# A transformer block and an RWKV/convolution block on one core: feed-forward activation sums behind the next products, GpSimd's 1024-column operations in two halves, the convolution norm's sums at a later place on TensorE

## The chip, the core and the metric

The kernel runs on 1 core of one Trainium2 chip. Its time is the device time of one execution in microseconds (us); lower is better. The engines are TensorE (PE, with its weight loads as PEld), VectorE (DVE), ScalarE (ACT), GpSimd (POOL) and SyncE (SP, which here only issues DMAs). Each has a queue of instructions that it works off in order; they meet through semaphores.

## What is computed

Two blocks stand one behind the other on 512 tokens of 1024 channels, all in f32. The first has two layers, each an attention mixer, a layer norm, a feed-forward with a squared ReLU, another layer norm and a gated embedding. The second is an RWKV-7 mixer beside a convolution branch, then a feed-forward of the same form. What the change touches is this:

```python
def _sq_relu_mlp(x, w_up, w_down):                 # layers 0 and 1: 1024 -> 4096 -> 1024
    return jnp.square(jax.nn.relu(x @ w_up)) @ w_down
...
    x = x + jnp.square(jax.nn.relu(h2 @ w_ff1[l])) @ w_ff2[l]      # second block
...
def _layernorm(x, g, b):                           # in the convolution branch
    mu = jnp.mean(xf, axis=-1, keepdims=True)
    var = jnp.mean(jnp.square(xf - mu), axis=-1, keepdims=True)
    y = (xf - mu) * lax.rsqrt(var + LN_EPS)
```

## The kernel before, in words

**Splits.** Each f32 operand is split into a rounded part `hi` and a rest `lo`, and a product is three matmuls, hi·hi, hi·lo and lo·hi (`mm3`, L290 to L292). A weight arrives by DMA in a tile `wraw` of 128x1024 (`load_part`, L261), ScalarE copies it to `whi`, and the rest `wlo` is made in one of three ways: VectorE or GpSimd subtracts (L273 in `load_part`, L389 in `split_sb`), or ScalarE negates and a DMA adds (L270, L271).

**Feed-forward** (`ffn`, three times: from about 225, 930 and 2115 us on). The 4096 hidden columns are worked off in 16 pieces of 256. `up(i)` makes one piece: two products of 24 matmuls each into PSUM (`psm`, two banks), and for each ScalarE applies ReLU (L440) and square (L441) into the tile `F` (`hf`, 128 x 8 x 256). From `F` VectorE makes four sums of blocks (L448 to L451; L451 needs L449's result), ScalarE rounds blocks 0 to 2 and blocks 3 to 6 into `hh` (L388, 128x768 and 128x1024), and VectorE makes the rests `hl` (L389). `F` has one buffer: the next piece's ReLU waits until the last rest of the piece before has been read.

`down(u)` multiplies two pieces with 512 rows of the second weight by a scheme of seven block products, for which GpSimd makes four sums of weight quarters (L488, L489, L490, L493, each 128x1024) and some of the rests. The products go through four PSUM banks `psa`; VectorE adds each result to `x` (L458, L460) or to a partial sum `q` (L505) and so frees its bank. The last 512 rows are done plainly (`down_last`).

**Order of the work.** The source is not the order of execution: the framework's scheduler places the instructions on each engine by its own estimate of their times, and the queues then run in that order. The order listings below show it.

**Convolution norm.** The convolution branch's layer norm (`ConvNorm`) sums eight tiles over the channels on GpSimd while they are made (L1345); `mean` is one matmul with ones (L1350) into the single PSUM bank `psd`. `center` then takes the eight tiles in turn: load from DRAM, subtract on GpSimd (L1357), store, square on ScalarE (L1359), add on GpSimd (L1363). `var` is a second matmul with ones into `psd` (L1368), a root on ScalarE and a reciprocal on VectorE. `sums()` (L1179) steps through these in stage 7 of `second_mixer`, woven by `interleave` with the other streams of that stage; a `yield` gives the weight of a step, and the number in `work += [(12.7, sums())]` sets the pace. `norm` then overwrites the shared activations `H` with the result, which is possible once the last of stage 8's gate products (`branch_gate`, also in `psd`) has read them. Beside all this runs `wkv_chunks`, a recurrence of eight steps for each of eight column groups; one step goes from TensorE (`psq`, L1416) to VectorE (L1655) to TensorE (L1661) to VectorE (L1663) to TensorE and to VectorE (L1675).

Of the kernel before, what the change touches and what calls it, by code (L numbers as in the profile page):

```python
# [11 lines left out]
F32 = mybir.dt.float32  # L12
F32R = mybir.dt.float32r
AF = mybir.ActivationFunctionType
ALU = mybir.AluOpType
# [185 lines left out]
class Ctx:  # L201
# [59 lines left out]
    def load_part(self, ap, raw, hi, lo, eng):  # L261

        nc = self.nc
        m = ap.shape[0] // 128 * ap.shape[1]
        nc.sync.dma_start(raw[:, :m].rearrange("p (k n) -> p k n", n=ap.shape[1]),
                          ap.rearrange("(k p) n -> p k n", p=128))
        nc.scalar.activation(hi[:, :m], raw[:, :m], AF.Copy)  # L267
        if eng is None:

            nc.scalar.activation(lo[:, :m], hi[:, :m].bitcast(F32), AF.Copy, scale=-1.0)  # L270
            nc.gpsimd.dma_start(lo[:, :m].bitcast(F32), raw[:, :m], accum_op=ALU.add)  # L271
        else:
            eng.tensor_tensor(lo[:, :m], raw[:, :m], hi[:, :m].bitcast(F32), op=ALU.subtract)  # L273

    def psum(self, st, **tags):

# [109 lines left out]

def split_sb(g, src, hi, lo, eng=None):
    g.nc.scalar.activation(hi, src, AF.Copy)  # L388
    (eng or g.nc.gpsimd).tensor_tensor(lo, src, hi.bitcast(F32), op=ALU.subtract)  # L389


def split_ps(g, ps, hi, lo):
# [10 lines left out]
def ffn(g, w_up, w_down, X, alpha, hp, tmp, late, norm, fm=None, fill=None):  # L403

    nc = g.nc
    V = nc.vector
    units = w_up.shape[1] // 512
    h = []
    seen = set()
    Q1 = [g.ps("psu") for _ in range(2)]
    QS = {k: hp.tile([128, 2, 512], F32, name=f"q{k}", tag=f"q{k}", bufs=1) for k in (5, 6, 7)}

    def first_two(W):

        pss = [g.ps("psa") for _ in range(2)]
        for half, t in enumerate(HALF_TOKENS):
            for e, ps in enumerate(pss):
                for kc in range(8):
                    w = tuple(a[:, e * 128:e * 128 + 128] for a in W[kc])
                    mm3(nc, ps[:, t], w, (X[0][:, kc, t], X[1][:, kc, t]), kc == 0, kc == 7)
                if half == 0:
                    late[e]()
        return pss

    def up(i):

        plain = i // 2 == units - 1
        W = g.load_w(w_up[:, i * 256:i * 256 + 256], eng=nc.gpsimd if i > 1 else None)
        F = tmp.tile([128, 8, 256], F32, name="hf", tag="hf")
        pss = first_two(W) if i == 0 else None
        for e in range(2):
            p3 = (pss[e] if pss else proj_fm(g, W, X, e * 128)).rearrange("p (a t) -> p a t", a=2)
            o = F[:, 1:3, :] if e else F[:, 0:8:7, :]
            nc.scalar.activation(o, p3, AF.Relu)  # L440
            nc.scalar.activation(o, o, AF.Square)  # L441
        hh = hp.tile([128, 7, 256], F32R, name="hh", tag="hh")
        hl = hp.tile([128, 7, 256], F32R, name="hl", tag="hl")
        split_sb(g, F[:, 0:3, :], hh[:, 0:3, :], hl[:, 0:3, :], V)
        if plain:
            split_sb(g, F[:, 7, :], hh[:, 3, :], hl[:, 3, :], V)
        else:
            V.tensor_tensor(F[:, 3, :], F[:, 7, :], F[:, 2, :], op=ALU.add)  # L448
            V.tensor_tensor(F[:, 4, :], F[:, 3, :], F[:, 0, :], op=ALU.subtract)  # L449
            V.tensor_tensor(F[:, 5, :], F[:, 0, :], F[:, 7, :], op=ALU.subtract)  # L450
            V.tensor_tensor(F[:, 6, :], F[:, 1, :], F[:, 4, :], op=ALU.subtract)  # L451
            split_sb(g, F[:, 3:7, :], hh[:, 3:7, :], hl[:, 3:7, :], V)
        h.append((hh, hl))

    def add(tb, c, ps):
        xs = g.x[tb][:, c * 512:c * 512 + 512]
        if (tb, c) not in seen and alpha != 1.0:
            V.scalar_tensor_tensor(xs, xs, alpha, ps, op0=ALU.mult, op1=ALU.add)  # L458
        else:
            V.tensor_tensor(xs, ps, xs, op=ALU.add)  # L460
        seen.add((tb, c))

    def down(u):
        q = w_down[u * 512:u * 512 + 512, :].rearrange("(j e p) n -> e p j n", e=2, p=128)
        new = lambda: g.wraw.tile([128, 1024], F32, name="wraw", tag="wraw")

        def quarter(e, c):
            t = new()
            nc.sync.dma_start(t.rearrange("p (j n) -> p j n", j=2), q[e][:, :, c * 512:c * 512 + 512])
            return t  # L470

        def parts(t, eng=None):
            hi = g.whi.tile([128, 1024], F32R, name="whi", tag="whi")
            lo = g.wlo.tile([128, 1024], F32R, name="wlo", tag="wlo")
            split_sb(g, t, hi, lo, eng)
            return hi, lo

        def product(W, k, ps, first=True, last=True):
            for t in range(2):
                for j in range(2):  # L480
                    x = tuple(a[:, k, t * 128:t * 128 + 128] for a in h[2 * u + j])
                    w = tuple(a[:, j * 512:j * 512 + 512] for a in W)
                    mm3(nc, ps[t], x, w, first and j == 0, last and j == 1)

        b11, b21, b12, b22 = quarter(0, 0), quarter(1, 0), quarter(0, 1), quarter(1, 1)
        B11, B21 = parts(b11), parts(b21)
        t3 = new()
        nc.gpsimd.tensor_tensor(t3, b22, b12, op=ALU.subtract)  # L488
        nc.gpsimd.tensor_tensor(b12, b12, b11, op=ALU.subtract)  # L489
        nc.gpsimd.tensor_tensor(b11, b22, b12, op=ALU.subtract)  # L490
        T2, T1, T3 = parts(b11), parts(b12, V), parts(t3, V)
        B22 = parts(b22, V)
        nc.gpsimd.tensor_tensor(b21, b21, b11, op=ALU.subtract)  # L493
        T4 = parts(b21)

        for k, W in ((1, B11), (2, B21), (6, T2), (5, T1), (7, T3), (3, B22), (4, T4)):
            ps = Q1 if k == 1 else [g.ps("psa") for _ in range(2)]
            product(W, BLOCK[k], ps, k > 1 or u == 0, k > 1 or u == units - 2)
            for t in range(2):
                if k in QS:  # L500
                    q = QS[k][:, t, :]
                    if u == 0:
                        nc.scalar.copy(q, ps[t])
                    else:
                        V.tensor_tensor(q, q, ps[t], op=ALU.add)  # L505
                elif k > 1:
                    add(2 * (k == 4) + t, int(k == 3), ps[t])

    def combine(ts):

        for t in ts:
            q5, q6, q7 = (QS[k][:, t, :] for k in (5, 6, 7))
            add(t, 0, Q1[t])
            V.tensor_tensor(q6, q6, Q1[t], op=ALU.add)
            V.tensor_tensor(q7, q7, q6, op=ALU.add)
            V.tensor_tensor(q6, q6, q5, op=ALU.add)
            V.tensor_tensor(q5, q5, q7, op=ALU.add)
            add(t, 1, q6)
            add(2 + t, 0, q7)
            add(2 + t, 1, q5)  # L520

    def down_last(u):
        for c in range(2):
            W = g.load_w(w_down[u * 512:u * 512 + 512, c * 512:c * 512 + 512], eng=nc.gpsimd)
            for tb in range(4):
                ps = g.ps("psa")
                for kc in range(4):
                    k = (kc % 2, 3 - kc % 2)[tb // 2]
                    x = tuple(a[:, k, tb % 2 * 128:tb % 2 * 128 + 128] for a in h[2 * u + kc // 2])
                    mm3(nc, ps, x, W[kc], kc == 0, kc == 3)  # L530
                add(tb, c, ps)
                if (c, tb) == (0, 1):
                    combine((1,))
                if c == 1:
                    norm(tb)
                    if fm and tb > 1:
                        fm(tb - 2)

    up(0)
    up(1)  # L540
    for u in range(units - 1):
        up(2 * u + 2)
        down(u)
        if u == units - 2:
            combine((0,))
        up(2 * u + 3)
    down_last(units - 1)
    if fill:
        fill()
    return [functools.partial(fm, tb) for tb in (2, 3)] if fm else None  # L550
# [574 lines left out]
def second_mixer(g, outer):  # L1125
    nc, tc, d = g.nc, g.tc, g.d
    H = g.X
    with ExitStack() as st:
# [12 lines left out]
        o = 0  # L1141
# [12 lines left out]
        with ExitStack() as s2, ExitStack() as s3, ExitStack() as s4:  # L1154
# [22 lines left out]
            outs = iter(range(8))  # L1177

            def sums():  # L1179
                yield 0.0  # L1180
                cn.mean()
                yield 4.0
                for j in range(8):
                    cn.center(j, ka)
                    yield 1.0
                cn.var()

            def conv_out(n):
# [52 lines left out]
            for i in range(1, 9):  # L1241
# [3 lines left out]
                late = [(10.0, wkv_inverse(g, i - 2, parts[i - 2], env))] if i > 1 else []  # L1245
                late += [(17.0, wkv_chunks(g, i - 3, parts[i - 3], env))] if i > 2 else []
                if i == SUMS:
                    work += [(12.7, sums())]
                interleave(*late, *work[::-1], (n, branches(i)))
            s4.close()  # L1250
            cn.pool = g.pool(s4, "wkc", 4, side="right")
# [506 lines left out]
```

## Time and profile before

| | |
|---|---|
| median of 3 executions | 2481.47 us (2478.55 to 2486.14) |
| the profiled execution | 2481.95 us |
| its span, first to last instruction | 2479.8 us |
| PE busy | 2364.9 us (95%) |
| DVE busy | 1481.9 us (60%) |
| ACT busy | 1283.0 us (52%) |
| POOL busy | 1030.6 us (42%) |
| mean granted TensorE clock | 0.984 of full |

Busy time is the sum of an engine's instructions, waits for operands inside an instruction included. The clock is the share of TensorE's full rate that was granted; it has two levels, 1.2 and 2.4 GHz, so 0.5 in a stretch is the lower one throughout.

### The profile page before, as it was taken

The numbers are of one execution on the slowest core, as the hardware profiler recorded it, in microseconds if no ns is written. First come the engines' busy times: TensorE is split into PE (matmuls) and PEld (weight loads), VectorE is DVE, ScalarE is ACT, GpSimd is POOL, SyncE is SP. The second block draws the span as 40 slices with busy tenths as digits, with TensorE's granted clock in tenths as the row PEclk, the third lists the DMA queues.
The fourth block names the chain that finished last, engine by engine and source line by source line (L and its number), as shares of the span: only waits on it lengthen the run. The fifth ranks groups of instructions, "written<-read, shape, count | busy, mean of one in ns | idle before, by whom it ended". The sixth has DMA issues, their size and how long they took to land.

```text
span 2479.8 us, 36415 instructions
## 1 busy us (share of the span) xinstructions
PE 2364.9 (95%) x14140; PEld 1898.6 (77%) x14140; DVE 1481.9 (60%) x2782; ACT 1283.0 (52%) x2005; POOL 1030.6 (42%) x571
## 2 busy tenths in 40 slices
PE   8999999999999999999999999999988999899998
PEld 6779778787777787877777877777766679787786
DVE  3776565666443655564685587877756542645556
ACT  5774454445465645444455454666655533544443
POOL 1114677662111025767632232323253114476772
PEclk9999999999999999999999999999998999999999
DMA  7445232347565244232372576666664468232322
GB/s 209 94 141 166 85 116 71 115 121 172 140 136 117 62 124 121 71 119 86 103 202 85 118 167 146 147 144 150 134 173 119 124 172 248 77 102 85 119 81 73
DMA packets 302349, 312.19 MB, mean 126 GB/s; under 512 B 61280, under 2 KB 234976, under 8 KB 302048
## 3 DMA queue, kind: packets, MB, share of 16 engines
q1 hardware_dynamic: 280432, 239.60, 31.9%
q0 software_dynamic: 21168, 68.17, 15.2%
q8 instruction: 111, 1.82, 0.3%
q10 hardware_dynamic: 576, 2.10, 0.2%
q14 instruction: 62, 0.51, 0.1%
HBM read 221.47 MB, written 20.19 MB: 97 GB/s over the span
## 4 chain that ended last, share of the span: by engine, by line
PE 55%; POOL 13%; issue 11%; DVE 9%; DMA 6%; ACT 6%; SPq 0%; POOLq 0%; DVEq 0%; ACTq 0%
PE psm L290 7%; PE psm L291 7%; PE psm L292 7%; POOL wlo L389 4%; PE psa L290 4%; PE psa L291 4%; PE psa L292 4%; POOL wlo L273 3%; DMA wlo<-wraw 2%; PE pst L1416 2%; PE psd L290 2%; PE pss L292 2%; PE pss L291 2%; PE pss L290 2%; PE psd L292 2%
## 5 line engine op out<-in xcount | busy, mean ns | idle before, releaser
L290 PE MATMUL psm<-xT,whi 128*128 128x512 f32 (+1 forms) x1192 | 476.2, 400 | 23.3 <-ACT hf L440 12.3
L292 PE MATMUL psm<-xT,wlo 128*128 128x512 f32 (+1 forms) x1192 | 469.7, 394 | 5.4 <-DMA wlo<-wraw 5.4
L291 PE MATMUL psm<-xT,whi 128*128 128x512 f32 (+1 forms) x1192 | 471.0, 395 | 0.5 <-DVE xT L352 0.5
L267 ACT ACTIVATE whi<-wraw 128x1024 fp32r<-128x1024 f32 (+3 forms) x287 | 285.7, 1005 | 290.8 <-PE psa L292 101.5
L271 POOL DMA_DIRECT2D wlo<-wraw x147 | 127.3, 872 | 729.0 <-ACT wlo L270 497.4
L273 POOL TENSOR_TENSOR wlo<-wraw,whi 128x1024 fp32r<-128x1024 f32 x122 | 315.5, 2620 | 102.0 <-ACT whi L267 73.4
L389 POOL TENSOR_TENSOR wlo<-wraw,whi 128x1024 fp32r<-128x1024 f32 x84 | 212.9, 2534 | 241.9 <-ACT whi L388 241.9
L290 PEld LDWEIGHTS psm<-xT,whi 128*128 128x128 f32 x1192 | 226.7, 190 | 74.7 <-ACT hf L440 13.6
L292 PEld LDWEIGHTS psm<-xT,wlo 128*128 128x128 f32 x1192 | 226.6, 190 | 53.1 <-DMA wlo<-wraw 6.5
L291 PEld LDWEIGHTS psm<-xT,whi 128*128 128x128 f32 x1192 | 227.4, 191 | 44.6 <-DVE xT L352 0.9
L290 PE MATMUL psa<-whi,hh 128*128 128x512 f32 x600 | 239.0, 398 | 15.6 <-DVE x L460 15.5
L291 PE MATMUL psa<-wlo,hh 128*128 128x512 f32 x600 | 236.6, 395 | 0.0
L292 PE MATMUL psa<-whi,hl 128*128 128x512 f32 x600 | 236.4, 395 | 0.0
L388 ACT ACTIVATE whi<-wraw 128x1024 fp32r<-128x1024 f32 x147 | 151.7, 1053 | 123.9 <-PE psa L292 61.8
L1407 DVE SCALAR_TENSOR_TENSOR psc<-glu,cw,psc 128x512 f32<-128x512 f32 x232 | 173.8, 749 | 5.9 <-ACT psc L1403 2.2
L388 ACT ACTIVATE hh<-hf 128x768 fp32r<-128x768 f32 (+1 forms) x96 | 87.8, 914 | 145.2 <-DVE hf L451 143.4
L389 DVE TENSOR_TENSOR hl<-hf,hh 128x768 fp32r<-128x768 f32 (+1 forms) x96 | 124.3, 1295 | 60.2 <-ACT hh L388 60.2
L290 PEld LDWEIGHTS psa<-whi,hh 128*128 128x128 f32 x600 | 112.8, 188 | 49.7 <-DVE x L460 23.1
L389 DVE TENSOR_TENSOR wlo<-wraw,whi 128x1024 fp32r<-128x1024 f32 x63 | 86.4, 1396 | 92.5 <-ACT whi L388 87.8
L270 ACT ACTIVATE wlo<-whi 128x1024 fp32r<-128x1024 f32 (+3 forms) x147 | 140.1, 956 | 2.3 <-PE psm L292 0.7
L292 PEld LDWEIGHTS psa<-whi,hl 128*128 128x128 f32 x600 | 112.8, 188 | 27.2 <-DVE hl L389 0.7
L291 PEld LDWEIGHTS psa<-wlo,hh 128*128 128x128 f32 x600 | 112.8, 188 | 25.8
(464 smaller groups left out, 5208.6 us busy)
## 6 DMA issues: line engine op xcount, KB each, us to landing
wlo<-wraw POOLq DMA_DIRECT2D x123, 512.0 KB, 5.3
wraw<-in_w_up SPq DMA_DIRECT2D x64, 512.0 KB, 4.5
wraw<-in_w_down SPq DMA_DIRECT2D x64, 512.0 KB, 3.6
wraw<-in_w_ff SPq DMA_DIRECT2D x64, 512.0 KB, 3.8
wraw<-in_w_in SPq DMA_DIRECT2D x56, 512.0 KB, 4.9
wraw<-in_od_w_in SPq DMA_DIRECT2D x24, 512.0 KB, 4.3
wraw<-in_ple_w_gate SPq DMA_DIRECT2D x16, 512.0 KB, 4.6
brow<-in_rows SPq DMA_DIRECT2D x13, 512.0 KB, 6.7
```

The source lines that it names most:

```text
L267: nc.scalar.activation(hi[:, :m], raw[:, :m], AF.Copy)
L270: nc.scalar.activation(lo[:, :m], hi[:, :m].bitcast(F32), AF.Copy, scale=-1.0)
L271: nc.gpsimd.dma_start(lo[:, :m].bitcast(F32), raw[:, :m], accum_op=ALU.add)
L273: eng.tensor_tensor(lo[:, :m], raw[:, :m], hi[:, :m].bitcast(F32), op=ALU.subtract)
L290: nc.tensor.matmul(ps, w[0], x[0], start=first, stop=False)
L291: nc.tensor.matmul(ps, w[0], x[1], start=False, stop=False)
L292: nc.tensor.matmul(ps, w[1], x[0], start=False, stop=last)
L388: g.nc.scalar.activation(hi, src, AF.Copy)
L389: (eng or g.nc.gpsimd).tensor_tensor(lo, src, hi.bitcast(F32), op=ALU.subtract)
L1407: nc.vector.scalar_tensor_tensor(acc if j == 30 else part, u[:, j:j + 512], cw[:, fc * 31 + j:fc * 31 + j + 1], part, op0=ALU.mult, op1=AL ...
L1416: nc.tensor.matmul(ps[o], lhs[o], rhs[o], start=start, stop=stop)
```

## The change

`up` no longer makes the sums and splits itself: it returns a function (`blocks`) that does, and the loop calls that function behind `down(u)` for the first piece of a pair and at once for the second. `F` gets two buffers. `on_gpsimd` issues a GpSimd operation on more than 512 columns in pieces of at most 512; it is used for the weights' rests and for the four sums of quarters. In the convolution norm the weights of the steps of `sums()` change.

```diff
@@ -270,7 +270,10 @@
             nc.scalar.activation(lo[:, :m], hi[:, :m].bitcast(F32), AF.Copy, scale=-1.0)
             nc.gpsimd.dma_start(lo[:, :m].bitcast(F32), raw[:, :m], accum_op=ALU.add)
         else:
-            eng.tensor_tensor(lo[:, :m], raw[:, :m], hi[:, :m].bitcast(F32), op=ALU.subtract)
+            if eng is nc.gpsimd:
+                on_gpsimd(nc, lo[:, :m], raw[:, :m], hi[:, :m].bitcast(F32), ALU.subtract)
+            else:
+                eng.tensor_tensor(lo[:, :m], raw[:, :m], hi[:, :m].bitcast(F32), op=ALU.subtract)

     def psum(self, st, **tags):

@@ -386,7 +389,18 @@

 def split_sb(g, src, hi, lo, eng=None):
     g.nc.scalar.activation(hi, src, AF.Copy)
-    (eng or g.nc.gpsimd).tensor_tensor(lo, src, hi.bitcast(F32), op=ALU.subtract)
+    if eng is None:
+        on_gpsimd(g.nc, lo, src, hi.bitcast(F32), ALU.subtract)
+    else:
+        eng.tensor_tensor(lo, src, hi.bitcast(F32), op=ALU.subtract)
+
+
+def on_gpsimd(nc, out, a, b, op):
+
+    n = out.shape[1]
+    for o in range(0, n, 512):
+        s = slice(o, min(o + 512, n))
+        nc.gpsimd.tensor_tensor(out[:, s], a[:, s], b[:, s], op=op)


 def split_ps(g, ps, hi, lo):
@@ -432,13 +446,16 @@

         plain = i // 2 == units - 1
         W = g.load_w(w_up[:, i * 256:i * 256 + 256], eng=nc.gpsimd if i > 1 else None)
-        F = tmp.tile([128, 8, 256], F32, name="hf", tag="hf")
+        F = tmp.tile([128, 8, 256], F32, name="hf", tag="hf", bufs=2)
         pss = first_two(W) if i == 0 else None
         for e in range(2):
             p3 = (pss[e] if pss else proj_fm(g, W, X, e * 128)).rearrange("p (a t) -> p a t", a=2)
             o = F[:, 1:3, :] if e else F[:, 0:8:7, :]
             nc.scalar.activation(o, p3, AF.Relu)
             nc.scalar.activation(o, o, AF.Square)
+        return functools.partial(blocks, F, plain)
+
+    def blocks(F, plain):
         hh = hp.tile([128, 7, 256], F32R, name="hh", tag="hh")
         hl = hp.tile([128, 7, 256], F32R, name="hl", tag="hl")
         split_sb(g, F[:, 0:3, :], hh[:, 0:3, :], hl[:, 0:3, :], V)
@@ -485,12 +502,12 @@
         b11, b21, b12, b22 = quarter(0, 0), quarter(1, 0), quarter(0, 1), quarter(1, 1)
         B11, B21 = parts(b11), parts(b21)
         t3 = new()
-        nc.gpsimd.tensor_tensor(t3, b22, b12, op=ALU.subtract)
-        nc.gpsimd.tensor_tensor(b12, b12, b11, op=ALU.subtract)
-        nc.gpsimd.tensor_tensor(b11, b22, b12, op=ALU.subtract)
+        on_gpsimd(nc, t3, b22, b12, ALU.subtract)
+        on_gpsimd(nc, b12, b12, b11, ALU.subtract)
+        on_gpsimd(nc, b11, b22, b12, ALU.subtract)
         T2, T1, T3 = parts(b11), parts(b12, V), parts(t3, V)
         B22 = parts(b22, V)
-        nc.gpsimd.tensor_tensor(b21, b21, b11, op=ALU.subtract)
+        on_gpsimd(nc, b21, b21, b11, ALU.subtract)
         T4 = parts(b21)

         for k, W in ((1, B11), (2, B21), (6, T2), (5, T1), (7, T3), (3, B22), (4, T4)):
@@ -536,14 +553,16 @@
                     if fm and tb > 1:
                         fm(tb - 2)

-    up(0)
-    up(1)
+    up(0)()
+    up(1)()
     for u in range(units - 1):
-        up(2 * u + 2)
+
+        later = up(2 * u + 2)
         down(u)
+        later()
         if u == units - 2:
             combine((0,))
-        up(2 * u + 3)
+        up(2 * u + 3)()
     down_last(units - 1)
     if fill:
         fill()
@@ -1177,12 +1196,13 @@
             outs = iter(range(8))

             def sums():
-                yield 0.0
+                yield 2.0
                 cn.mean()
                 yield 4.0
                 for j in range(8):
                     cn.center(j, ka)
                     yield 1.0
+                yield 3.0
                 cn.var()

             def conv_out(n):
@@ -1245,7 +1265,7 @@
                 late = [(10.0, wkv_inverse(g, i - 2, parts[i - 2], env))] if i > 1 else []
                 late += [(17.0, wkv_chunks(g, i - 3, parts[i - 3], env))] if i > 2 else []
                 if i == SUMS:
-                    work += [(12.7, sums())]
+                    work += [(17.5, sums())]
                 interleave(*late, *work[::-1], (n, branches(i)))
             s4.close()
             cn.pool = g.pool(s4, "wkc", 4, side="right")
```

What becomes of it on the engines' queues, at three places (names are those of the tiles; a row's number of executions in sequence is behind the x):

ScalarE, in the first feed-forward, from the first piece's rounded blocks to the third piece's ReLU, with the semaphores that each row waits for; before:

```order
L388 ACTIVATE hh<-hf 128x1024 [waits DVE_49]
L440 ACTIVATE hf<-psm 128x2x256 [waits DVE_49,PE_49]
L441 ACTIVATE hf<-hf 128x2x256 [waits Activation_49]
L388 ACTIVATE whi<-wraw 128x1024 [waits PE_49,Pool_49]
L388 ACTIVATE whi<-wraw 128x1024 [waits DMAHW7_49,PE_49]
L440 ACTIVATE hf<-psm 128x512 [waits PE_49]
```

and of the change:

```order
L391 ACTIVATE hh<-hf 128x1024 [waits DVE_49]
L454 ACTIVATE hf<-psm 128x2x256 [waits PE_49]
L455 ACTIVATE hf<-hf 128x2x256 [waits Activation_49]
L391 ACTIVATE whi<-wraw 128x1024 [waits PE_49,Pool_49]
L391 ACTIVATE whi<-wraw 128x1024 [waits DMAHW7_49,PE_49]
L454 ACTIVATE hf<-psm 128x512 [waits PE_49]
```

The order is the same, and the ReLU no longer waits for VectorE; the rounding of the earlier piece's last four blocks (`hh` 128x1024) still stands ahead of it. The rows of VectorE and TensorE in the feed-forwards stand in the same order as before, too.

GpSimd, in the first feed-forward, from `down(0)` on; before:

```order
L488 TENSOR_TENSOR wraw<-wraw 128x1024
L489 TENSOR_TENSOR wraw<-wraw 128x1024
L389 TENSOR_TENSOR wlo<-wraw,whi 128x1024
L490 TENSOR_TENSOR wraw<-wraw 128x1024
L389 TENSOR_TENSOR wlo<-wraw,whi 128x1024
L493 TENSOR_TENSOR wraw<-wraw 128x1024
```

and of the change:

```order
L403 TENSOR_TENSOR wraw<-wraw 128x512 x4
L403 TENSOR_TENSOR wlo<-wraw,whi 128x512 x2
L403 TENSOR_TENSOR wraw<-wraw 128x512 x2
L403 TENSOR_TENSOR wlo<-wraw,whi 128x512 x2
L403 TENSOR_TENSOR wraw<-wraw 128x512 x2
```

The same six operations in the same order, each as two.

TensorE, around the matmul for the convolution norm's variance; before:

```order
L1416 MATMUL pst<-mm,yy 64x64 x16
L1416 MATMUL pst<-ar,bk 64x128 x8
L1368 MATMUL psd<-cnsq,ca 128x512
L1661 MATMUL psq<-s_16718,md_11247 128x64
...
L1580 MATMUL psm<-bon,cb 128x512
L290 MATMUL psd<-xT_61,whi 128x512
```

and of the change:

```order
L1681 MATMUL psq<-s_17211,md_11444 128x64
L1610 MATMUL pst<-ca,bk 128x128
L1436 MATMUL psq<-vtk,ktk 64x64 x2
...
L1436 MATMUL pso<-st,ar 64x64 x2
L1388 MATMUL psd<-cnsq,ca 128x512
L1681 MATMUL psq<-s_17257,md_11444 128x64
...
L1681 MATMUL psq<-s_17313,md_11444 128x64
L293 MATMUL psd<-xT_61,whi 128x512
```

Before, one step of the next recurrence stands between the variance and stage 8's gate products (`psd<-xT,whi`). Now six of that recurrence's eight steps stand ahead of the variance, with transposes and small products between them and no gate product, and the gates follow in blocks of 24 matmuls. The mean (L1350, now L1370) has moved too: from beside the second step of the recurrence of stage 7 to behind its last but one, ahead of the four transposes `pst<-ca,bk` (L1590, now L1610).

## Rows read from the trace of the kernel before

**Rows 1.** Who waited for whom, TensorE: total us, times, longest.

```profile
PE psa L290 <- DVE x L460: 15.5, 14, 1.7
PE psm L290 <- ACT hf L440: 12.3, 3, 4.7
...
PE psd L1368 <- POOL cnsq L1363: 4.1, 1, 4.1
...
PE psd L1350 <- POOL cnsum L1345: 1.8, 1, 1.8
```

**Rows 2.** Timeline of TensorE (start, us; idle before, releaser), the three feed-forwards' starts.

```profile
255.72 0.65 PE L290 MATMUL psm<-xT,whi 128*128 128x512 f32 x1 [4.19 <-ACT hf L440]
...
961.38 0.50 PE L290 MATMUL psm<-xT,whi 128*128 128x512 f32 x1 [3.35 <-ACT hf L440]
...
2148.79 0.80 PE L290 MATMUL psm<-xT,whi 128*128 128x512 f32 x1 [4.74 <-ACT hf L440]
```

**Rows 3.** Stretches: length, busy us of PE, PEld, DVE, ACT, POOL; clock; DMA.

```profile
255.00:262.00 7.00, 6.28 (x21) 5.06 (x22) 4.08 (x5) 5.08 (x7) 2.39 (x1) 0.76 0.14 36
961.00:968.00 7.00, 6.62 (x22) 5.27 (x23) 4.41 (x5) 4.81 (x7) 2.39 (x1) 0.76 0.18 53
2148.00:2155.00 7.00, 6.21 (x17) 4.92 (x18) 4.05 (x6) 5.07 (x7) 2.39 (x1) 0.59 0.12 31
...
1820.00:1834.00 14.00, 9.26 (x76) 6.71 (x77) 10.30 (x28) 3.54 (x9) 6.28 (x5) 0.76 0.33 98
1860.00:1874.00 14.00, 13.04 (x75) 10.15 (x76) 9.03 (x19) 9.81 (x14) 3.65 (x4) 0.63 0.15 42
```

**Rows 4.** Timeline of ScalarE, the same start of the first feed-forward.

```profile
252.66 1.06 ACT L388 ACTIVATE hh<-hf 128x1024 fp32r<-128x1024 f32 x1 [8.57 <-DVE hf L451]
255.07 0.60 ACT L440 ACTIVATE hf<-psm 128x512 f32<-128x512 f32 x1 [1.35 <-DVE hl L389]
```

**Rows 5.** Timeline of VectorE, ahead of it.

```profile
243.24 1.27 DVE L448 TENSOR_TENSOR hf<-hf 128x256 f32<-128x256 f32 x1 [1.28 <-ACT hf L441]
244.54 2.50 DVE L449 TENSOR_TENSOR hf<-hf 128x256 f32<-128x256 f32 x1
246.97 3.15 DVE L389 TENSOR_TENSOR hl<-hf,hh 128x768 fp32r<-128x768 f32 x1
250.03 2.60 DVE L451 TENSOR_TENSOR hf<-hf 128x256 f32<-128x256 f32 x1
253.75 1.23 DVE L389 TENSOR_TENSOR hl<-hf,hh 128x1024 fp32r<-128x1024 f32 x1 [1.12 <-ACT hh L388]
```

**Rows 6.** Instructions on the tile hf: duration min/median/max in ns, first and last start.

```profile
L389 DVE TENSOR_TENSOR hl<-hf,hh x96: 416/959/3159, 247.0 to 2450.8; 128x768 fp32r<-128x768 f32 x48, 128x1024 fp32r<-128x1024 f32 x42, 128x256 fp32r<-128x256 f32 x6
...
L449 DVE TENSOR_TENSOR hf<-hf x42: 424/426/2518, 244.5 to 2411.6; 128x256 f32<-128x256 f32 x42
```

**Rows 7.** Timeline of GpSimd around 230 us.

```profile
225.78 5.60 POOL L273 TENSOR_TENSOR wlo<-wraw,whi 128x1024 fp32r<-128x1024 f32 x2 [0.67 <-ACT whi L267]
```

**Rows 8.** Timeline of VectorE beside it.

```profile
226.30 2.81 DVE L374 SCALAR_TENSOR_TENSOR x<-x,bmv,brow 128x512 f32<-128x512 f32 x1
```

**Rows 9.** Instructions on the tile cnsq: GpSimd's 512-column operation.

```profile
L1363 POOL TENSOR_TENSOR cnsq<-cnsq,cn x7: 1263/1275/1290, 1819.9 to 1859.6; 128x512 f32<-128x512 f32 x7
```

**Rows 10.** Timeline of VectorE in down(1).

```profile
317.58 2.24 DVE L389 TENSOR_TENSOR hl<-hf,hh 128x1024 fp32r<-128x1024 f32 x1 [0.53 <-ACT hh L388]
319.74 0.68 DVE L460 TENSOR_TENSOR x<-psa,x 128x512 f32<-128x512 f32 x1
```

**Rows 11.** Timeline of TensorE in down(1).

```profile
320.48 0.50 PE L290 MATMUL psa<-whi,hh 128*128 128x512 f32 x1 [0.96 <-DVE x L460]
```

**Rows 12.** Timeline of TensorE in the convolution stretch: mean, transposes, variance, a step.

```profile
1803.69 0.70 PE L1350 MATMUL psd<-cnsum,ca 128*128 128x512 f32 x1 [1.81 <-POOL cnsum L1345]
...
1834.16 0.66 PE L1590 MATMUL pst<-ca,bk 128*128 128x128 f32 x4
...
1860.96 2.07 PE L1368 MATMUL psd<-cnsq,ca 128*128 128x512 f32 x2 [4.10 <-POOL cnsq L1363]
...
1951.48 0.33 PE L1661 MATMUL psq<-s,md 128*128 128x64 f32 x2
...
1954.47 0.43 PE L1661 MATMUL psq<-s,md 128*128 128x64 f32 x2
```

## The prediction

> **What bounds the kernel now.** I read the engines' shares first: TensorE is busy for 2364.9 of 2479.8 us, no other engine for more than 60%. Time can only come from TensorE's idle stretches, about 115 us in all, and from stretches in which its clock is low. The second view, who waited for whom on TensorE, says which idle time the change can touch [rows 1]: in the feed-forwards 12.3 us in three waits for the ReLU (`hf`, L440) and 15.5 us in 14 waits for VectorE's additions into `x` (L460); in the convolution stretch 1.8 us ahead of the mean and 4.1 us ahead of the variance. The third view, the timeline, shows that the three long waits for `hf` are one per feed-forward, near its start, of 4.19, 3.35 and 4.74 us [rows 2]. The fourth, stretches with their granted clock, shows what follows such a wait: 0.76, 0.76 and 0.59 over 7 us behind the heads, 0.63 over 14 us behind the variance [rows 3]. TensorE had been idle just before each fall.
>
> Why is the ReLU late? In the first head ScalarE stood idle 8.57 us for VectorE's sum L451 before it could round `hh`, then 1.35 us for the rest `hl`, since `F` has one buffer; only then came the ReLU at 255.07 [rows 4]. VectorE had no idle time to speak of in between: it spent 1.27, 2.50, 3.15 and 2.60 us on four operations [rows 5], of which the small one normally takes 0.42 (the median of L449) and the 768-column one 0.96 (the median of the 768- and 1024-column rests together, the nearest I have) [rows 6]. The four took 9.52 us instead of 3 x 0.42 + 0.96 = 2.22, so 7.3 us are waiting inside VectorE's instructions. I read that as waiting for GpSimd: both read two operands from SBUF. The piece of evidence is a pair of GpSimd operations from 225.78 to 231.38 without a gap, beside a VectorE operation that took 2.81 us and ended at 229.11, while the second of the pair ran [rows 7, 8]. So VectorE gets in between two GpSimd operations that touch, but not inside one; one operation of 1024 columns there is 5.60/2 = 2.80 us.
>
> **The change, part by part.** The sum is made against the profiled execution, 2481.95 us, 0.5 above the median of the three; they differ by up to 7.6 us among themselves, so that the two can't be told apart. No difference under 0.3% (7.4 us) can be.
>
> *Halves and the ReLU at the heads.* A GpSimd operation on 512 columns takes 1.275 us [rows 9], so a VectorE operation that waits one out now loses at most that. The four operations then take at most 2.22 + 4 x 1.275 = 7.3 us (at least 2.2 less than 9.52), and with arrivals in the middle of an operation, half of it each, 4.8 (4.7 less). The ReLU besides no longer waits for `hl`: 1.35 earlier [rows 4]. The rounding `hh` still stands ahead of it on ScalarE and still waits for L451, so it can't come earlier than that. A head thus gains 2.2 + 1.35 = 3.6 at least and 6.1 at most, where 4.19, 3.35 and 4.74 are at stake. I take 0.35 left at each, for the case between: 12.3 - 1.1 = **-11.2**. Bounds: -4 (only the 1.35 each) and -12.3.
>
> *The clock behind the heads.* At the granted clock 7 x 0.24 + 7 x 0.24 + 7 x 0.41 = 6.2 us are lost there [rows 3]. If TensorE doesn't stand still, the clock has no cause to fall: **-5.5**; bounds 0 and -6.2.
>
> *The additions into x.* TensorE waits 14 times, 1.1 us on average, for a bank that L460 frees. In one such place VectorE's queue has the rest `hl` with 2.24 us, 1.0 of it over the 1.23 that it takes when free [rows 5, 10], then L460 with 0.68, then TensorE goes on after 0.96 idle [rows 10, 11]. VectorE's order is the same in the change, so L460 still stands behind `hl`; what comes earlier is `hl` itself (a wait on a half is 0.64 on average, where the 2.80 us of a whole gave 1.4) and the ReLU chain, by up to 1.35. Either alone covers most of 1.1. I take **-12** of 15.5; bounds -3 and -15.5. That the source calls the sums behind `down(u)` I cost at nothing: in the listings the queues' order doesn't show it.
>
> *More GpSimd instructions.* Two halves are 2 x 1.275 = 2.55 us where one was 2.80 beside VectorE [rows 7, 9]: **0**. Even 0.1 more for each would lie in GpSimd's idle 58%. If that cover were gone the weight's rest `wlo` would be late for its 24 matmuls; its first half now is there earlier.
>
> *The convolution norm.* The mean moves from 1803.69 to just ahead of the transposes `ca,bk`, which ran at 1834.16 [rows 12]. Its wait goes: -1.8. GpSimd's work for `center` leaves the stretch from 1820 to 1834, where TensorE was busy for 9.26 of 14 us at a clock of 0.76 [rows 3]: 4.7 idle and 14 x 0.24 = 3.4 of clock, together 8.1. The recurrence is there in any case, so I take half: -4. Against this the next recurrence's six steps now stand without gate products between them. A step by itself comes every 2.99 us [rows 12]; with the transposes and small products that stand between I take 1 us of idle time a step, so +6 (bounds 0 and 12). The variance: mean to variance took 57.3 us (1803.69 to 1860.96) [rows 12]. With the mean at about 1834 - 5 = 1829 it would be ready by 1886 if the chain takes as long, while TensorE gets there at 1861 - 4.1 - 1.8 + 6 x 2.99 = 1873: a wait of up to 13. Both ends are far apart (0 and 13); I take the nearest row, the old wait of 4.1 with its clock (14 x 0.37 = 5.2), so that old and new cancel. Sum -1.8 - 4 + 6 = **0**; bounds -17 (no new wait, no bare steps) and +16 (steps 6, a wait of 13 with a clock loss like the old one's 5.2 against the 9.3 that went, and nothing of the 8.1: 6 + 18.2 - 9.3 - 1.8 = 13; with steps at 9, 16). Behind the variance in TensorE's queue stand the gate products, so nothing fills that wait; `norm`, which needs them, would only follow later.
>
> Sum: -11.2 - 5.5 - 12 + 0 = -28.7, so **2453**.
>
> **The rivals.**
>
> *Halves buy VectorE nothing (0.14).* If a half passes the port to the half behind it without a gap, VectorE waits as long as before. For it: L448 to L451 wait for 2.5 us and more in a row, as if for whole operations [rows 5]. Against it: VectorE's end at 229.11, inside a GpSimd pair [rows 7, 8]. Then heads gain 3 x 1.35 = 4, the clock stays, the additions gain 8 by the second buffer: 2482 - 12 = 2470.
> The Trainium skill, page "GPSIMD Engine Reference", section "2.1 Instruction dispatch", speaks for this rival: consecutive GpSimd instructions are no barrier between its eight cores, each of which starts on the next instruction as soon as it is done with its own share of the last. By that the two halves would run into each other like one operation; the trace disagrees as far as [rows 7, 8] go, with VectorE's end at 229.11 between 225.78 and 231.38.
>
> *The change doesn't do what it says at the additions (0.15).* The order of VectorE's queue is unchanged, and `hl` is still ahead of L460. If the 14 waits are set by that order, and not by how long `hl` waits, they stay but for 3 us: 2453 + 9 = 2462. For it: L460 itself took only 0.68 [rows 10]; against: 1.0 us of `hl` ahead of it was waiting.
>
> *The variance late (0.12), or so late that the change loses (0.07).* The wait of 13 us worked out above puts the convolution term at +13: 2466. It loses from a certain point: each us by which the variance comes after 1873 costs one, and about half a us more at the low clock behind it. To eat 28.7, the wait would have to cost 28.7 + 9.3 = 38, that is about 25 us (ready at 1898, 12 us more than the 57 of before). That happens if the recurrence's VectorE operations, now in a bunch, hold GpSimd's `center` up: 1.275 an operation when free [rows 9], sixteen of them. If the chain takes 79 us instead of 57, the wait is 35 and costs 52: 2453 + 43 = 2496. Against it: the wait of before was only 4.1 with the same chain.
>
> **How the numbers follow.** The forecast has 0.52, with 2436 to 2461 as its own range. Beside it 0.14 at 2470, 0.15 at 2462, 0.12 at 2466 and 0.07 around 2496. The range 2435 to 2475 leaves out the last and some 0.12 at both ends of the others. Faster by over 0.3% (under 2474): 0.52 + 0.15 + most of 0.14 and 0.12, together 0.85. Within 0.3%: 0.09. Slower: 0.06.
>
> **What would show it.** Heads with under 1 us of waiting for `hf` and a clock of 0.95 or more behind them; longest L449 about 1.7 us where it was 2.52; L460's waits under 5 us in sum; GpSimd's halves at 1.2 to 1.3 us; a wait ahead of the variance of 0 to 8 us. It would be wrong if L449 still takes 2.5 us, if the L460 waits stay over 10 us, or if TensorE stands over 20 us ahead of the variance.

## The result and the profile after

The changed kernel takes 2446.24 us (median of 4 executions, 2445.41 to 2449.20) against 2482.09 of the kernel before (4 executions): a ratio of 0.9857, interval 0.984 to 0.9875, some 36 us faster. The prediction said 2453 in 2435 to 2475. The profiled execution's span is 2445.0 us where it was 2479.8.

The first line of the page:

```profile
PE 2351.4 (96%) x14140; PEld 1894.8 (77%) x14140; DVE 1468.9 (60%) x2782; ACT 1280.3 (52%) x2005; POOL 1106.1 (45%) x866
```

GpSimd is some 75 us busier than before. TensorE's waits (total us, times, longest) that answer to [rows 1]:

```profile
PE psa L293 <- DVE x L477: 8.7, 16, 0.9
...
PE psd L1388 <- POOL cnsq L1383: 4.0, 1, 4.0
```

The line for `hf` is gone: the heads don't wait at all. The additions' waits (now L477) are down by 6.8 us, the variance's (now L1388) is as long as it was, the mean's is gone. The rows below give the clock at the three heads, where [rows 3] showed 0.76, 0.76 and 0.59 (length, then busy us of PE, PEld, DVE, ACT, POOL, then the clock). The matmuls that waited there now start at 250.18, 946.52 and 2119.39, and each stretch begins within 5 us of one:

```profile
248.00:255.00 7.00, 7.00 (x33) 5.79 (x32) 6.44 (x4) 5.50 (x8) 7.00 (x5) 1.00 0.01 2
951.00:958.00 7.00, 7.00 (x32) 5.77 (x32) 5.84 (x7) 2.51 (x4) 2.93 (x2) 1.00 0.41 133
2116.00:2123.00 7.00, 7.00 (x32) 5.75 (x31) 5.87 (x5) 5.32 (x8) 7.00 (x5) 1.00 0.00 0
```

From 217 to 610, 877 to 1290 and 2112 to 2436 us, the whole of the three feed-forwards, the clock is 1.00 as well.

VectorE and ScalarE at the first head, to be held against [rows 4, 5]:

```profile
242.06 0.55 DVE L465 TENSOR_TENSOR hf<-hf 128x256 f32<-128x256 f32 x1 [2.15 <-ACT hf L455]
242.64 1.40 DVE L466 TENSOR_TENSOR hf<-hf 128x256 f32<-128x256 f32 x1
243.96 2.05 DVE L395 TENSOR_TENSOR hl<-hf,hh 128x768 fp32r<-128x768 f32 x1
245.92 1.51 DVE L468 TENSOR_TENSOR hf<-hf 128x256 f32<-128x256 f32 x1
...
247.47 1.06 ACT L391 ACTIVATE hh<-hf 128x1024 fp32r<-128x1024 f32 x1 [4.56 <-DVE hf L468]
248.43 0.58 ACT L454 ACTIVATE hf<-psm 128x512 f32<-128x512 f32 x1
```

The four operations take 5.5 us instead of 9.5, ScalarE stands idle 4.56 us instead of 8.57, and the ReLU (L454) follows `hh` at once.

Where the 34.4 us between the first and the last matmul's start went, by the starts of the same matmuls (the n-th of 14140) in both traces:

| stretch | change | predicted |
|---|---|---|
| first feed-forward (matmuls 1250 to 3000) | -9.5 us | |
| second (4250 to 6250) | -10.2 us | |
| third (12750 to 14139) | -10.0 us | together -28.7 us |
| convolution norm (10000 to 11500) | -8.8 us | 0 |
| all the rest | +4.0 us | 0 |

The rest, in which the order of the program is the same in all but a few rows, is the clock falling at other places: TensorE's idle time there is 1.5 us shorter than before. In the convolution stretch, the 1500 matmuls of the last row but one, kernel before and then the change:

```profile
1792.30:1969.20 176.90, 156.98 (x1504) 114.93 (x1503) 102.53 (x301) 94.51 (x175) 64.75 (x55) 0.89 0.53 138
```

```profile
1776.50:1944.60 168.10, 147.27 (x1501) 110.42 (x1499) 98.14 (x297) 94.53 (x174) 65.18 (x54) 0.93 0.55 144
```

TensorE idles for 176.90 - 156.98 = 19.9 us before and 20.8 now. The idle time has moved and has not shrunk; what is gone is time at the low clock: 0.11 x 176.9 = 19.5 us lost before, 0.07 x 168.1 = 11.8 now, 7.7 of the 8.8 us.

### The profile page after: what moved, and what is told of

Same layout as the page of the kernel before. It is cut to its first block, busy times and chain, and to the rows that moved or that the text cites. A ratio compares the mean times of both kernels' runs of the same rounds, so it can differ in the third digit from the quotient of the medians.

```text
span 2445.0 us, 36669 instructions
## 1 busy us (share of the span) xinstructions
PE 2351.4 (96%) x14140; PEld 1894.8 (77%) x14140; DVE 1468.9 (60%) x2782; ACT 1280.3 (52%) x2005; POOL 1106.1 (45%) x866
## 3 DMA queue, kind: packets, MB, share of 16 engines
q8 instruction: 111, 1.82, 0.3%
## 4 chain that ended last, share of the span: by engine, by line
PE 53%; POOL 14%; issue 11%; DMA 8%; DVE 7%; ACT 6%; SPq 0%; POOLq 0%; DVEq 0%; ACTq 0%
POOL wlo L403 9%; PE psm L293 6%; PE psm L295 6%; PE psm L294 6%; PE psa L293 4%; POOL wraw L403 4%; PE psa L294 4%; PE psa L295 4%; DMA wlo<-wraw 3%; PE pss L293 2%; PE pst L1436 2%; PE pss L295 2%; PE pss L294 2%; PE psd L293 2%; PE psd L295 2%
## 5 line engine op out<-in xcount | busy, mean ns | idle before, releaser
L403 POOL TENSOR_TENSOR wlo<-wraw,whi 128x512 fp32r<-128x512 f32 x412 | 576.2, 1433 | 257.7 <-ACT whi L391 161.7
L403 POOL TENSOR_TENSOR wraw<-wraw 128x512 f32<-128x512 f32 x168 | 243.9, 1477 | 40.4 <-DMA wraw<-in_w_down 28.3
L395 DVE TENSOR_TENSOR hl<-hf,hh 128x768 fp32r<-128x768 f32 (+1 forms) x96 | 148.8, 1549 | 67.6 <-ACT hh L391 67.6
L294 PEld LDWEIGHTS psa<-wlo,hh 128*128 128x128 f32 x600 | 113.0, 188 | 25.6
```

Source lines behind the costliest of these rows:

```text
L294: nc.tensor.matmul(ps, w[0], x[1], start=False, stop=False)
L395: eng.tensor_tensor(lo, src, hi.bitcast(F32), op=ALU.subtract)
L403: nc.gpsimd.tensor_tensor(out[:, s], a[:, s], b[:, s], op=op)
```

## The experiments

All are edits of the kernel before or of the changed kernel, each with its ratio to the kernel before, run beside it. The theory behind them: the heads were late because VectorE waits out a GpSimd operation, and the halves shorten that; the second buffer takes the wait for `hl` away; the norm's order gives clock.

### One part of the change at a time

**Two buffers alone.** In the kernel before:

```diff
-        F = tmp.tile([128, 8, 256], F32, name="hf", tag="hf")
+        F = tmp.tile([128, 8, 256], F32, name="hf", tag="hf", bufs=2)
```

> The kernel before with two buffers for F and nothing else. Theory (the heads are late because VectorE's sums wait out whole GpSimd operations; the buffer is the smaller part): the heads keep most of their 12.3 us of waiting, less 1.35 each, so about 8; the clock still falls behind at least one of them; the additions lose some 3 of their 15.5 us; about 2475 us. Rival (the wait was for the buffer: nothing can go on until F has been read): heads nearly free, additions down to 9, about 2457 us.

Measured: 2460.62 us, ratio 0.9912 (0.9898 to 0.9926), near the rival's 2457 and 14 us better than the theory said. Its waits:

```profile
PE psm L290 <- ACT hf L440: 8.3, 3, 3.3
```

The heads stand as the theory expected, at 8.3 us. The additions don't: no wait for L460 is left at all, where the kernel before had 15.5 us. So the one buffer, and not the halves, cleared the additions. One such wait stood at 405.89 in the kernel before:

```profile
395.26 0.60 ACT L440 ACTIVATE hf<-psm 128x512 f32<-128x512 f32 x1 [1.35 <-DVE hl L389]
405.16 0.68 DVE L460 TENSOR_TENSOR x<-psa,x 128x512 f32<-128x512 f32 x1
405.89 0.50 PE L290 MATMUL psa<-whi,hh 128*128 128x512 f32 x1 [1.16 <-DVE x L460]
```

The same two operations with two buffers:

```profile
392.15 0.58 ACT L440 ACTIVATE hf<-psm 128x512 f32<-128x512 f32 x1
402.01 0.68 DVE L460 TENSOR_TENSOR x<-psa,x 128x512 f32<-128x512 f32 x1
```

Counted from the start of the 72nd matmul ahead of the waiting one (388.01 before, 386.19 here), the ReLU comes after 7.25 us before and after 5.96 here. VectorE's operations behind that ReLU in the pair of pieces are 1.3 us earlier too, the addition included (17.15 and 15.82 us). TensorE starts the matmul ahead of the wait at 16.3 in both, and here goes on without standing still.

**Halves alone.** In the kernel before, `on_gpsimd` with its two calls as in the change, one buffer, the old sums.

> The kernel before with GpSimd's operations in halves and nothing else (one buffer for F, the norm's sums as before). Theory: the four operations of VectorE ahead of the first head's ReLU take 5 to 7 us instead of 9.5, the heads wait for 1 to 2 us each (the ReLU still waits for the rest hl, 1.35), the additions some 10 us; about 2463 us. Rival (a half hands the port to the next half, VectorE gains nothing): heads 12 us, additions 15, 2482 us. Rival of the buffer: 2480.

Measured: 2487.92 us, ratio 1.0025 (1.0014 to 1.0035): slower, where the theory said 20 us faster. Its waits:

```profile
PE psa L293 <- DVE x L474: 25.6, 20, 1.8
...
PE psm L293 <- ACT hf L454: 4.5, 3, 1.8
```

At the heads the halves do what was said of them: 4.5 us instead of 12.3, and by the same matmuls TensorE has gained 5.5, 5.7 and 5.7 us just behind them, counted from the start of each of the three stretches of the table. But over the rest of each stretch it loses that again, and ends 2.1, 0.2 and 0.5 us behind the kernel before: the additions' waits rise from 15.5 to 25.6 us.

**The norm's sums alone.** In the kernel before:

```diff
-                yield 0.0
+                yield 2.0
                 cn.mean()
...
+                yield 3.0
                 cn.var()
...
-                    work += [(12.7, sums())]
+                    work += [(17.5, sums())]
```

> The kernel before with the later sums of the convolution norm and nothing else. Theory (the 8 us that the changed kernel gains between 1790 and 1970 are clock: idle time of TensorE there is about 20 us in both, the time at the low clock 38 us before and 24 after): about 2474 us, the idle time unchanged within 2 us, the wait ahead of the variance still about 4 us. Rival (they come from the halved GpSimd work of that stretch, not from the order): 2482 us within 3.

Measured: 2475.03 us, ratio 0.9967 (0.9956 to 0.9979), so 8 us as the theory said. The same 1500 matmuls:

```profile
1799.30:1966.00 166.70, 145.63 (x1500) 109.83 (x1500) 101.52 (x297) 94.55 (x174) 63.63 (x54) 0.94 0.55 145
```

Idle 21.1 us, clock 0.94: here too only the clock has changed. The wait ahead of the variance, which was to stay at 4 us, is 0.2 in this run; the waits for a step of the recurrence are longer instead. That the mean's first `yield` alone makes this order can be read from the queues as built: with 0.0 there, and all else as in the change, the mean and the variance stand where they stood before; with 1.0, 2.0 or 4.0 the order is that of the change, whatever number stands ahead of the variance or sets the pace.

**No halves.** The changed kernel with whole GpSimd operations:

```diff
-    for o in range(0, n, 512):
-        s = slice(o, min(o + 512, n))
+    for o in range(0, n, 1024):
+        s = slice(o, min(o + 1024, n))
```

> The changed kernel with GpSimd's 1024-column operations whole again (two buffers, later sums). Theory (the buffer alone clears the additions, the halves only help at the heads): waits for x under 1 us, heads 8 us as with the buffer alone, 2450 to 2454 us, that is 4 to 8 us slower than the change. Rival (the halves are what matters in the changed kernel): over 2458 us.

Measured: 2449.42 us, ratio 0.9868 (0.9848 to 0.9888). The waits are the theory's:

```profile
PE psm L293 <- ACT hf L454: 9.6, 3, 3.7
```

and 0.2 us in all for the additions. In time the halves are worth 0.9868 - 0.9857 = 0.1% of the kernel, less than the theory's 4 to 8 us, and the intervals overlap: most of what they save at the heads they give back behind them.

**No deferral.** The changed kernel with the sums called at once for both pieces:

```diff
-        later = up(2 * u + 2)
+        up(2 * u + 2)()
         down(u)
-        later()
```

> The changed kernel with the sums called at once for both pieces (two buffers kept). Theory (the scheduler gives the same order on every queue, so the deferral is nothing): 2446 us within 3, waits as in the change. Rival (the deferral counts, by where buffers lie or by other waits): 5 us or more slower.

Measured: 2447.02 us, ratio 0.9852 (0.9834 to 0.9869), the change's own within the error, with the same 8.7 us of waits for `x`. The scheduler gives all five queues the same order either way, and the deferral has no part in the result.

### Why the halves cost time behind the heads

**Quarters.** The changed kernel with pieces of 256 columns, `range(0, n, 256)`.

> The changed kernel with pieces of 256 columns instead of 512. Theory (each VectorE operation waits out one GpSimd piece): the four sums of blocks, which now take 0.93 to 1.5 us as medians where 0.42 is their free time, fall to 0.7 to 0.9; the additions' 8.7 us of waiting fall to 3 to 5; 2441 to 2444 us. Rival (a GpSimd operation has a fixed cost, so that four pieces cost much more than two, and the weights' rests come late): pieces of 256 take over 0.8 us, TensorE waits for wlo, 2450 us or more.

Measured: 2500.41 us, ratio 1.0059 (1.0038 to 1.0079): 54 us slower than with halves. In time that is the rival's side, but its reasons hold only in part: a piece takes 0.74 us, and TensorE waits for the additions and for `hl`, hardly for GpSimd's `wlo` (1.4 us in four waits of `psa`).

```profile
PE psa L293 <- DVE x L477: 25.6, 32, 1.1
PE psu L295 <- DVE hl L395: 19.7, 12, 1.7
```

GpSimd's sums of quarters, (minimum/median/maximum ns), in the change and with quarters:

```profile
L403 POOL TENSOR_TENSOR wraw<-wraw x168: 1278/1298/2290, 237.1 to 2376.7; 128x512 f32<-128x512 f32 x168
```

```profile
L403 POOL TENSOR_TENSOR wraw<-wraw x336: 722/739/1738, 237.9 to 2430.2; 128x256 f32<-128x256 f32 x168
```

and whole, in the kernel before:

```profile
L488 POOL TENSOR_TENSOR wraw<-wraw x21: 2390/2405/2419, 236.8 to 2395.6; 128x1024 f32<-128x1024 f32 x21
```

1024 columns cost 2.40 us in one piece, 2.60 in two and 2.96 in four. That isn't all of the 54 us: the twelve waits for `hl` each end some 1.7 us behind a VectorE operation that took 7.3 us instead of 1.22 (last section), so this run doesn't price the pieces alone.

A run of seven such operations in the steady state, in the next experiment's kernel (whole there) and in the change (start, us, line, tiles, count):

```profile
407.35 4.88 POOL L403 TENSOR_TENSOR wraw<-wraw 128x1024 f32<-128x1024 f32 x2 [1.48 <-DMA wraw<-in_w_down]
412.18 2.40 POOL L403 TENSOR_TENSOR wlo<-wraw,whi 128x1024 fp32r<-128x1024 f32 x1
414.66 2.45 POOL L403 TENSOR_TENSOR wraw<-wraw 128x1024 f32<-128x1024 f32 x1
...
422.79 2.57 POOL L403 TENSOR_TENSOR wlo<-wraw,whi 128x1024 fp32r<-128x1024 f32 x1
```

```profile
408.95 3.79 POOL L403 TENSOR_TENSOR wraw<-wraw 128x512 f32<-128x512 f32 x3 [1.21 <-DMA wraw<-in_w_down]
412.70 2.54 POOL L403 TENSOR_TENSOR wlo<-wraw,whi 128x512 fp32r<-128x512 f32 x2
415.19 3.96 POOL L403 TENSOR_TENSOR wraw<-wraw 128x512 f32<-128x512 f32 x3
...
425.28 3.44 POOL L403 TENSOR_TENSOR wlo<-wraw,whi 128x512 fp32r<-128x512 f32 x2
```

The run takes 425.36 - 407.35 = 18.0 us whole and 428.72 - 408.95 = 19.8 us in halves. In its middle ScalarE waits for the sum to round it, ahead of the next ReLU in its queue, whole first:

```profile
412.74 0.60 ACT L454 ACTIVATE hf<-psm 128x512 f32<-128x512 f32 x1 [4.33 <-PE psm L295]
...
417.14 2.01 ACT L391 ACTIVATE whi<-wraw 128x1024 fp32r<-128x1024 f32 x2 [3.14 <-POOL wraw L403]
...
426.88 1.06 ACT L391 ACTIVATE hh<-hf 128x1024 fp32r<-128x1024 f32 x1 [5.70 <-DVE hf L468]
```

```profile
414.01 0.60 ACT L454 ACTIVATE hf<-psm 128x512 f32<-128x512 f32 x1 [4.25 <-PE psm L295]
...
419.18 2.01 ACT L391 ACTIVATE whi<-wraw 128x1024 fp32r<-128x1024 f32 x2 [3.91 <-PE psm L294]
...
429.03 1.06 ACT L391 ACTIVATE hh<-hf 128x1024 fp32r<-128x1024 f32 x1 [5.81 <-DVE hf L468]
```

Counted from the ReLU, `whi` starts after 4.40 us and after 5.17, and the rounded blocks `hh` after 14.14 and after 15.02: 0.9 us later with halves. (The change's row names TensorE as the releaser; the GpSimd sum it also needs ended at 415.19 + 3.96 = 419.15, right before it.) Of the 0.77 us by which `whi` is later, the longer run of GpSimd has 0.44: from its start to the end of the sum it takes 9.76 us whole and 10.20 in halves. The other 0.33 are that the run starts later, behind a DMA; why it does was not followed. The next ReLU stands behind `hh`, and the addition at the end of the chain (`x`, L477) starts 24.99 us after the first ReLU whole and 25.99 in halves; TensorE then waits 0.68 us for it in halves and not at all whole.

**Halves only at the heads.** The changed kernel, with halves for the four sums and the rests of `down(0)` alone:

```diff
-            split_sb(g, t, hi, lo, eng)
+            split_sb(g, t, hi, lo, eng, 1024 if u else 512)
...
-        on_gpsimd(nc, t3, b22, b12, ALU.subtract)
+        on_gpsimd(nc, t3, b22, b12, ALU.subtract, 1024 if u else 512)
```

and so for the other three; `load_part` whole. The last argument is the width of a piece.

> The changed kernel with halves only in down(0) of each feed-forward, whole operations everywhere else. Theory (halves pay where GpSimd's operations stand back to back ahead of the second piece's ReLU, and cost in the steady state, where they delay the sums of the next pieces): no wait for hf at the heads, waits for x under 1 us where the change has 8.7, 2436 to 2440 us. Rival (the additions' 8.7 us have nothing to do with the halves, or the heads wait for GpSimd's loads too): 2446 us or more.

Measured: 2436.99 us (2436.51 to 2437.83), ratio 0.9812 (0.9798 to 0.9827), clear of the change's 0.9857 (0.984 to 0.9875), and as the theory said; the norm's order is that of the change. No wait for `hf` is left, and of the waits for the additions and the variance these:

```profile
PE psa L293 <- DVE x L477: 0.5, 1, 0.5
...
PE psd L1388 <- POOL cnsq L1383: 0.4, 1, 0.4
```

This version beats both kernels, the one before by 1.9%.

## Why the prediction was right, and where it was not

**The heads, predicted -11.2, were 12.3.** The mechanism was the one named: four VectorE operations that each wait out a GpSimd operation, shortened by the halves to 5.5 us (4.8 to 7.3 predicted), and the ReLU that no longer waits for `hl`. With either part alone 4.5 or 8.3 us of the wait stay, so it takes both. The parts don't simply add: alone, buffer, halves and norm order change the time by -22, +5 and -8 us, together by -36, and beside the second buffer the halves no longer cost time on balance ("No halves").

**The clock behind them, -5.5, was 6.2:** 1.00 in all three stretches.

**The additions, -12, were 6.8.** This term was mis-sized, and its reason failed. "Half of a wait" didn't come: `hl` in down(1) and its like take 2.37 us in the change, 1.14 of it waiting, where [rows 10] had 2.24, 1.0 of it waiting. What cleared the additions was the ReLU, 1.3 us earlier by the second buffer. That alone takes all 15.5 us away, and the halves put 8.7 back.

**More GpSimd instructions, 0, is the step that failed.** I priced the whole operation at 2.80 us, from a pair in contention [rows 7], against 2 x 1.275 for the halves. As medians it is 2.40 (the first sum of quarters) against 2.60. I looked for the cost at `wlo` and in GpSimd's idle share; in the pair of pieces followed above it came at ScalarE's rounding of the sums, which stands ahead of the next ReLU. Over the kernel GpSimd's 1024-column work took 750 us whole and 839 in halves, summed over its 290 operations.

**The convolution norm, 0, was -8.8,** inside its bounds of -17 and +16. In the profiled execution the wait of the variance took the place of the old one as forecast, 4.0 for 4.1 us, but that was luck: without the deferral, with the same order on every queue, it is 0.2 us, in the other four kernels with this order 0.4 or less, and the waits for the steps of the recurrence are longer instead (5.5 to 8.9 us for `st`, where the change has 3.2). The steps that stand without gate products cost as much idle time as the mean's and the other waits had; the idle sum of the stretch is 19.9 and 20.8 us. The clock is what the term left out: I let the loss behind the variance stand and took half of that at 1820. Over the same 1500 matmuls the clock was 0.89, 0.89 and 0.92 in the three kernels with the old order and 0.93 to 0.95 in the six with the new, with 18.6 to 22.2 us idle throughout, and the kernel with the sums alone is 8 us faster by its times too. So the order brings it; why the same idle time at other places costs less of clock isn't settled.

**The sum.** The traces are 34.4 us apart where 28.7 was predicted. The errors, 5 us too much at the additions and 9 too little at the norm, partly cancelled; heads and clock gave 2 us more than forecast, and 4 went to the clock elsewhere. That leaves 4 us: of the 29.7 in the three stretches of the feed-forwards no term of the sum has 4.4. Two waits for VectorE ahead of the heads account for 1.2 and 1.0 of them: TensorE waits 1.45 us for L352 at 233.24 before and 0.26 at 232.06 in the change, and 0.78 for L389 at 889.45 before and not at all now. The halves bring these two: with halves alone they are as short, and every kernel whose `load_part` stays whole keeps them. A further 1.5 us was low clock at 932 in the kernel before, behind a wait of 1.82 us that is as long in the change, and 0.6 the part of the third fall ahead of the stretch in [rows 3]. So the feed-forwards came out 1 us from the forecast by errors that cancelled, and the time 7 us below it.

**The rivals.** That halves buy VectorE nothing is refuted at the heads: the longest wait of a VectorE sum falls from 2.22 to 1.15 us (durations of 168 sums, 96 rests `hl` and 81 rests `wlo`, each less the shortest of its shape). It holds in another way, though: these waits add up to 143 us in the kernel before and 153 in the change, over 0.3 us in 84 operations before and in 140 now. Halving made them shorter and more. At the first head all four operations had waited, and 9.5 us became 5.5. In the pair of pieces shown above they take 2.62, 2.50, 0.95 and 0.41 us whole and 1.51, 1.39, 2.04 and 1.51 in halves: 6.5 us either way.
The Trainium skill, page "SBUF — State Buffer", section "Who interferes with whom", says that a VectorE instruction with two SBUF inputs contends with a GpSimd instruction that reads SBUF, and that the lock on the ports they share is exclusive. The trace agrees for wholes and halves, with longest waits of 2.22 and 1.15 us beside operations of 2.40 and 1.30. The long waits with quarters, below, it doesn't explain.

That the change doesn't do what it says at the additions was half right: the deferral did nothing (0.9852 without it), and the waits didn't go as far as forecast. The variance wasn't late: the chain from mean to variance took 47.8 us (1808.11 to 1855.94), not 57:

```profile
1808.11 1.10 PE L1370 MATMUL psd<-cnsum,ca 128*128 128x512 f32 x2 [0.41 <-ACT bgt L1338]
...
1855.94 2.08 PE L1388 MATMUL psd<-cnsq,ca 128*128 128x512 f32 x2 [3.95 <-POOL cnsq L1383]
```

## What to carry to other kernels

Cutting an operation that another engine has to wait out made each wait shorter here, not the sum of them, and the pieces cost more than the whole. It paid where each of several operations in a row on the path had waited out a whole one, and cost time elsewhere; so look for such places and cut there alone. Price the pieces against the uncontended whole, and follow the cutting engine's later results to the engine that waits for them in order, even if the cutting engine is idle half of the time. Where a stage waits for the last reader of a one-buffer tile, try the second buffer by itself first; and a call moved in the source is a change only if the queues as built show it.

## What was not expected of the hardware

With quarters VectorE's small sums hardly wait (medians of 0.42 to 0.46 us), but twelve of its 1024-column rests, those in the downs, take some 6.1 us more than their 1.22, each beside an unbroken run of GpSimd pieces:

```profile
435.26 7.30 DVE L395 TENSOR_TENSOR wlo<-wraw,whi 128x1024 fp32r<-128x1024 f32 x1 [8.28 <-POOL wlo L403]
```

```profile
433.08 2.83 POOL L403 TENSOR_TENSOR wlo<-wraw,whi 128x256 fp32r<-128x256 f32 x4
435.88 2.80 POOL L403 TENSOR_TENSOR wraw<-wraw 128x256 f32<-128x256 f32 x4
438.65 2.82 POOL L403 TENSOR_TENSOR wlo<-wraw,whi 128x256 fp32r<-128x256 f32 x4
```

The operation ends 1.1 us after the run's end at 441.47, as if it had been let in only then, past eight pieces' ends. So do the other eleven, and a thirteenth of 4.53 us: each ends 1.1 us after the end of the GpSimd run beside it. Thirteen more rests that also start inside such a run take only 1.7 us. With halves no wait is over 1.15 us. What tells the two kinds apart stays open. And the clock: two stretches with the same work and 20 us of idle time each were granted 0.89 and 0.93, that is, 8 us apart.
